# FoX queries and keys made token-major and turned through DRAM, in a two-layer mLSTM and FoX trunk

## The chip, the cores and the metric

The kernel runs on one core of one Trainium2 chip. The metric is device time in microseconds (us) of one execution; the times shown are of separate executions of the same program. A profile is one more execution, recorded by the hardware profiler. Engines are named as the profile does: PE is TensorE (PEld its weight loads), DVE is VectorE, ACT is ScalarE, POOL is GpSimd, SP is SyncE, whose queue issues nearly all loads.

## The reference

The input is x, 256 tokens by 2048 features in float32, with one conditioning vector c. Layer 0 mixes tokens with an mLSTM, layer 1 with FoX attention; each mixer is followed by a SwiGLU FFN (5632 wide). Before every mixer and FFN stands an RMSNorm with a scale and a shift that are computed from c, and every result is added to x through a gate computed from c. What the change touches most is the FoX mixer:

```
def forgetting_attention(q, k, v, log_f):          # 16 heads of 128
    cum = jnp.cumsum(log_f, axis=-1)
    s = jnp.einsum('bhqd,bhkd->bhqk', qi, kf) * scale + cqi[..., None] - cum[..., None, :]
    s = jnp.where(kpos[None, :] <= qpos[:, None], s, -jnp.inf)
    p = jax.nn.softmax(s, axis=-1)
    return jnp.einsum('bhqk,bhkd->bhqd', p, vf)

def fox_mixer(h, w_in, b_f, w_out):
    proj = h @ w_in                                # 2048 -> q, k, v of 2048 each, 16 gates
    ...
    return o.astype(h.dtype) @ w_out
```

and, at the very start, the modulation of layer 0, `mod = silu(c) @ ada_w + ada_b` with `h = rms_norm(x) * (1 + sc1) + sh1`.

## The kernel before, in words

**Products in three parts.** Every large product is a float32 product made of float32r matmuls. A weight block (four k tiles of 128 rows, 512 columns, 1 MB) is loaded by SP into a buffer `raw` (five of them), and in two halves ScalarE writes its rounded part `hi` (line 261) and VectorE the remainder `lo` (line 262); there are four buffers of each, so two blocks can be split ahead. The activations are kept feature-major as `hT`, for each k tile 256 columns of high parts and then 256 of low parts. A product is high x high + high x low + low x high.

**Two shapes of projection.** `group_a` (through `mm_a` and `mm_t`, lines 288 to 290) is token-major: activations are the weights of TensorE, the 512 weight columns move, and for each k tile there are two token halves of three matmuls of 512 columns; its result lies in two PSUM banks. `group_b` (through `mm_b`, lines 271 and 274) is feature-major: for each of four 128-column blocks the weights are stationary, and one matmul of 512 columns (hi against both parts of `hT`) and one of 256 (lo against the high part) follow; its result lies in four of the six banks of that pool, and `total` (lines 353, 355, 357) adds the two halves of a bank. Before the change, FoX q and k use `group_b`, because the score of a head needs q and k with features on the partitions; all other projections use `group_a`.

**Steps and ticks.** Small work is put in the list `steps`, and after each block of four k tiles `tick(n, adv)` takes `adv` steps from it; `drain()` takes all. The same tick lets `bg` start modulation tiles (`ada_tile`: a 1 MB load and one multiply-and-sum on VectorE, line 193) at a rate `FR` per tick. The tile scheduler then sets the order of each engine's queue; only the start, up to the first token-major products, is ordered by hand.

**A FoX head is three steps.** The score (lines 676, 681, 1201): logit bias and mask as bfloat16 matmuls, then q against k in plain float32, into one of the two `aux` banks; VectorE takes the maximum (1211), ScalarE the exponential (1216), VectorE the division by the sum (1223). The flip (922, 923): three 128 x 128 transposes of the weights through an aux bank. The mix (1233, 1236): values against weights, split into high and low for the output projection (362, 363). Four heads form a group, one for each projection of 512 columns of q and of k; their twelve steps are interleaved, all scores first. They become steps as soon as the group's k is there, and run in the ticks of the next projections, one a tick; before the next group's heads are added, `drain()` takes what is left. The output projection `project_out` takes two steps a tick and drains all before its k tile 12, since k tile h is head h.

**The last FFN's turn.** In layer 1 the hidden activations are turned without TensorE: VectorE transposes 32 x 32 squares (line 1128), POOL writes the result to a DRAM tile `aside` (1132) and reads it back rearranged (1136), and ScalarE and VectorE split it (1147, 1148) reading columns 16 bytes apart.

**The start.** SP loads x, then modulation tiles for scale and shift of each k tile, and, between them, 512 KB pairs of k tiles of the first four mLSTM projections (line 780). For k = 0 to 2 the unsplit activations (VectorE line 737, ScalarE line 741) go against unsplit weights in plain float32 (`full_k`, line 785); k = 3 is the first in three parts. `split_act` (362, 363) makes the high and low halves of each `hT` tile, `split_last` (797, 798) those of the weights for k = 3.

## Time and profile before

| what | us |
|---|---|
| three timed executions | 2286.4, 2284.6, 2287.0; median 2286.4 |
| profiled execution | 2287.6, its span 2285.6 |
| TensorE busy in the span | 2259.6 (99%) |
| VectorE, ScalarE, GpSimd busy | 1642.5, 1133.3, 53.8 |
| modulation tiles on VectorE (line 193, 192 of them) | 438.9 |
| low halves of weights on VectorE (line 262, 764) | 925.7 |

The busy time of TensorE counts matmuls whose durations overlap: one of 512 columns is listed with 391 ns, while the next begins after some 230. How fast TensorE goes is therefore read from starts in the timeline, and where it waits from the idle time in brackets behind an instruction. `PEclk` is the clock granted to TensorE as a share of full speed. In the windows view the columns are: stretch, its length, and for each engine the busy time with the number of instructions, then PEclk, the DMA engines' busy share and GB/s.

### The profile page before, as it was taken

To read this page: it belongs to the slowest core of one execution; us is meant where nothing else is said; L and a number is where in the kernel's file an instruction comes from. 1 tells how busy PE (TensorE), PEld (TensorE's weight loads), DVE (VectorE), ACT (ScalarE), POOL (GpSimd) and SP (SyncE) were. 2 spreads that over 40 slices of the span, in tenths; PEclk is the share of its full clock that TensorE was granted. 3 is DMA by queue.
4 is the path that set the end of the run, shared out by engine and by line. 5 is a ranking of instruction groups with operands and counts; after the bars stand their busy time and mean duration, and the time that the engine had idled before them with its cause. 6 is when DMAs were issued, how large, how long until landed. Compare 5 with 4: busy or idle time off the path is not lost.

```text
span 2285.6 us, 26531 instructions
## 1 busy us (share of the span) xinstructions
PE 2259.6 (99%) x10290; PEld 1853.0 (81%) x10290; DVE 1642.5 (72%) x1855; ACT 1133.3 (50%) x1493; POOL 53.8 (2%) x106
## 2 busy tenths in 40 slices
PE   8999999999999999999999999999999999999998
PEld 4877878888888888888888888888888888888886
DVE  7998789878877877865687777777666555555564
ACT  4778564555543344444554544455444443444443
POOL 1000000000000000000000000000010100010000
PEclk9999999999999999999999999999999999999999
DMA  9998989798888889985567878675787665566662
GB/s 386 369 354 332 350 307 355 281 342 336 324 330 332 323 332 342 340 299 185 212 251 277 310 261 293 240 271 195 256 288 254 221 204 189 198 226 217 206 228 104
DMA packets 91809, 635.44 MB, mean 278 GB/s; under 512 B 10962, under 2 KB 11410, under 8 KB 17316
## 3 DMA queue, kind: packets, MB, share of 16 engines
q1 hardware_dynamic: 86400, 617.79, 73.9%
q0 software_dynamic: 5136, 15.83, 2.4%
q8 instruction: 80, 1.31, 0.2%
q14 instruction: 45, 0.37, 0.0%
q10 hardware_dynamic: 148, 0.14, 0.0%
HBM read 625.82 MB, written 7.90 MB: 277 GB/s over the span
## 4 chain that ended last, share of the span: by engine, by line
PE 87%; DVE 6%; DMA 4%; ACT 2%; issue 1%; SPq 0%; POOL 0%; ACTq 0%; DVEq 0%; POOLq 0%
PE mm L290 25%; PE mm L289 25%; PE mm L288 25%; PE mm L271 5%; DMA ada<-in_ada_w_dram 3%; DVE ada L193 3%; PE mm L274 3%; DVE lo L262 2%; ACT hi L261 1%; PE aux L345 1%; PE aux L974 0%; PE aux L483 0%; PE aux L1201 0%; PE mm L554 0%; PE mm L550 0%
## 5 line engine op out<-in xcount | busy, mean ns | idle before, releaser
L262 DVE TENSOR_TENSOR lo<-raw,hi 128x1024 fp32r<-128x1024 f32 x764 | 925.7, 1223 | 488.6 <-ACT hi L261 487.9
L261 ACT CAST hi<-raw 128x1024 fp32r<-128x1024 f32 x764 | 795.6, 1052 | 881.3 <-PE mm L290 780.7
L289 PE MATMUL mm<-lo,hT 128*128 128x512 f32 x1846 | 721.1, 391 | 4.5 <-DVE lo L262 4.5
L288 PE MATMUL mm<-hi,hT 128*128 128x512 f32 x1846 | 720.4, 392 | 1.3 <-ACT hT L362 1.3
L290 PE MATMUL mm<-hi,hT 128*128 128x512 f32 x1846 | 720.8, 390 | 0.0
L193 DVE SCALAR_TENSOR_TENSOR ada<-ada,cs 128x2048 f32<-128x2048 f32 x192 | 438.9, 2286 | 52.4 <-DMA ada<-in_ada_w_dram 52.0
L289 PEld LDWEIGHTS mm<-lo,hT 128*128 128x128 f32 x1846 | 346.9, 188 | 79.1 <-DVE lo L262 8.6
L288 PEld LDWEIGHTS mm<-hi,hT 128*128 128x128 f32 x1846 | 346.6, 188 | 73.5 <-ACT hT L362 2.1
L290 PEld LDWEIGHTS mm<-hi,hT 128*128 128x128 f32 x1846 | 346.7, 188 | 72.7 <-issue 0.5
L288 PE MATMUL mm<-hi,slot 128*128 128x512 f32 x960 | 375.5, 391 | 0.2 <-ACT slot L1007 0.2
L289 PE MATMUL mm<-lo,slot 128*128 128x512 f32 x960 | 374.6, 390 | 0.0
L290 PE MATMUL mm<-hi,slot 128*128 128x512 f32 x960 | 374.6, 391 | 0.0
L290 PEld LDWEIGHTS mm<-hi,slot 128*128 128x128 f32 x960 | 180.3, 188 | 37.8 <-issue 0.7
L288 PEld LDWEIGHTS mm<-hi,slot 128*128 128x128 f32 x960 | 180.3, 188 | 37.7 <-ACT slot L1007 0.8
L289 PEld LDWEIGHTS mm<-lo,slot 128*128 128x128 f32 x960 | 180.4, 188 | 36.9
L271 PE MATMUL mm<-hT,hi 128*128 128x512 f32 x512 | 181.8, 402 | 0.9 <-DVE slot L357 0.9
L274 PE MATMUL mm<-hT,lo 128*128 128x256 f32 x512 | 138.4, 281 | 0.0
L271 PEld LDWEIGHTS mm<-hT,hi 128*128 128x128 f32 x512 | 94.5, 188 | 20.8 <-DVE slot L357 1.3
L274 PEld LDWEIGHTS mm<-hT,lo 128*128 128x128 f32 x512 | 96.8, 189 | 3.1
L829 ACT ACTIVATE slot<-mm 128x512 f32<-128x512 f32 x78 | 45.2, 595 | 39.2 <-PE mm L290 37.4
L1148 DVE TENSOR_TENSOR slot<-slot,slot 128x512 fp32r<-128x512 f32 x22 | 23.8, 1089 | 24.1 <-ACT slot L1147 24.1
L433 ACT ACTIVATE t<-X 128x512 f32<-128x512 f32 x32 | 20.1, 629 | 38.4 <-DVE X L428 38.4
(220 smaller groups left out, 1034.1 us busy)
## 6 DMA issues: line engine op xcount, KB each, us to landing
ada<-in_ada_w_dram SPq DMA_DIRECT2D x192, 1024.0 KB, 6.5
raw<-in_gate_up_dram SPq DMA_DIRECT2D x176, 1024.0 KB, 5.0
raw<-in_down_dram SPq DMA_DIRECT2D x88, 1024.0 KB, 4.8
raw<-in_fox_in_dram SPq DMA_DIRECT2D x48, 1024.0 KB, 4.9
raw<-in_w_in_dram SPq DMA_DIRECT2D x44, 1024.0 KB, 7.4
raw<-in_w_out_dram SPq DMA_DIRECT2D x16, 1024.0 KB, 6.5
raw<-in_fox_out_dram SPq DMA_DIRECT2D x16, 1024.0 KB, 4.9
aside<-slot POOLq DMA_DIRECT2D x22, 256.0 KB, 2.7
```

What stands on the lines that cost most here:

```text
L193: nc.vector.scalar_tensor_tensor(out=raw, in0=raw, scalar=1.0, in1=cs, op0=ALU.mult, op1=ALU.mult, accum_out=acc[layer][:, j : j + 1],)
L261: nc.scalar.copy(hi, raw[:, j : j + 2, :])
L262: nc.vector.tensor_tensor(lo, raw[:, j : j + 2, :], hi.bitcast(F32), op=ALU.subtract)
L271: nc.tensor.matmul(ps, hi, rhs, start=first, stop=last, skip_group_check=True)
L274: nc.tensor.matmul(ps[:, T:], lo, rhs[:, :T], start=False, stop=False, skip_group_check=True)
L288: nc.tensor.matmul(ps, a, hi, start=first, stop=False, skip_group_check=True)
L289: nc.tensor.matmul(ps, a, lo, start=False, stop=False, skip_group_check=True)
L290: nc.tensor.matmul(ps, b, hi, start=False, stop=last, skip_group_check=True)
L345: nc.tensor.transpose(ps[:, j * T + t * P : j * T + (t + 1) * P], src[:, t, (2 * i + j) * P : (2 * i + j + 1) * P], ident,)
L433: nc.scalar.activation(t512(), X[:, t, 512 * i : 512 * (i + 1)], AF.Square, accum_out=self.ss[:, t, i : i + 1],)
L829: nc.scalar.activation(SP[i][:, t, :], banks[t], func)
L1148: nc.vector.tensor_tensor(dst[:, :, T:], ps, dst[:, :, :T].bitcast(F32), op=ALU.subtract)
```

## The change

It does four things. (1) FoX q and k are projected token-major by `group_a`. ScalarE copies each token half out of its bank, with the scale; VectorE transposes its 32 x 32 squares; POOL writes them to DRAM and reads them back with four DMAs into a tile of 256 tokens by 4 heads on 128 feature partitions, the head innermost. The heads' score matmuls read that tile directly, so consecutive tokens of one head are 16 bytes apart. `blocks` and `gather` are the last FFN's functions, moved out. (2) A group's heads become steps only after the next group's q projection, and run in the next k projection, three steps a tick. The last v projection moves behind the last k, and the last heads run after it. (3) In the FoX output projection the first two column groups do k tiles 0 to 11 each, holding four banks, with two steps a tick; then what is left is drained and both do k tiles 12 to 15. (4) At the start, the low half of `hT` for k = 0 to 3 is made behind the next modulation tile's multiply instead of ahead of it, and the weight pairs are fetched in another order among the modulation tiles.

Three places in the engines' queues show it. The first is SP's queue at the start, before the change; `ada` is a modulation tile, `slot<-in_w_in_dram` a weight pair.

```order
L192 DMA ada_232<-in_ada_w_dram 128x2048
L780 DMA slot_242<-in_w_in_dram 128x1024
L780 DMA slot_244<-in_w_in_dram 128x1024
L780 DMA slot_246<-in_w_in_dram 128x1024
L780 DMA slot_248<-in_w_in_dram 128x1024
L192 DMA ada_258<-in_ada_w_dram 128x2048
L192 DMA ada_262<-in_ada_w_dram 128x2048
L192 DMA ada_280<-in_ada_w_dram 128x2048
L192 DMA ada_284<-in_ada_w_dram 128x2048
```

And with the change:

```order
L192 DMA ada_232<-in_ada_w_dram 128x2048
L806 DMA slot_241<-in_w_in_dram 128x1024
L806 DMA slot_243<-in_w_in_dram 128x1024
L192 DMA ada_245<-in_ada_w_dram 128x2048
L806 DMA slot_250<-in_w_in_dram 128x1024
L192 DMA ada_252<-in_ada_w_dram 128x2048
L806 DMA slot_261<-in_w_in_dram 128x1024
L192 DMA ada_279<-in_ada_w_dram 128x2048
L192 DMA ada_284<-in_ada_w_dram 128x2048
```

Modulation tile 2 (`ada_258`, now `ada_245`) has moved ahead of two pairs and tile 3 ahead of one; from tile 4 on the bytes ahead are the same, up to a swap of one pair with tile 6.

The second is VectorE's queue there, for k = 1, before the change (`mods` is one column of scale or shift, `t` the scaled activations, `hT` the low half):

```order
L363 TENSOR_TENSOR hT<-t_36_238,hT 128x256
L193 SCALAR_TENSOR_TENSOR ada_258,acc_124<-ada_258,cs 128x2048
L181 SCALAR_TENSOR_TENSOR mods_122<-acc_124,prm 128x1
L193 SCALAR_TENSOR_TENSOR ada_262,acc_124<-ada_262,cs 128x2048
L187 TENSOR_TENSOR mods_122<-acc_124,prm 128x1
L737 SCALAR_TENSOR_TENSOR t_43_266<-slot_130,mods_122,R 128x256
L363 TENSOR_TENSOR hT<-t_44_268,hT 128x256
L193 SCALAR_TENSOR_TENSOR ada_280,acc_124<-ada_280,cs 128x2048
```

And with the change:

```order
L193 SCALAR_TENSOR_TENSOR ada_245,acc_124<-ada_245,cs 128x2048
L759 TENSOR_TENSOR hT<-t_36_238,hT 128x256
L181 SCALAR_TENSOR_TENSOR mods_122<-acc_124,prm 128x1
L193 SCALAR_TENSOR_TENSOR ada_252,acc_124<-ada_252,cs 128x2048
L187 TENSOR_TENSOR mods_122<-acc_124,prm 128x1
L752 SCALAR_TENSOR_TENSOR t_42_256<-slot_130,mods_122,R 128x256
L193 SCALAR_TENSOR_TENSOR ada_279,acc_124<-ada_279,cs 128x2048
L759 TENSOR_TENSOR hT<-t_43_258,hT 128x256
```

The low half has moved behind the next tile's multiply.

The third is TensorE's queue around a head's score in the FoX stage, before the change (one score between blocks of a feature-major projection):

```order
L676 LDWEIGHTS sel
L676 MATMUL aux_9744<-u_1682_9245,sel 128x512
L681 LDWEIGHTS identb
L681 MATMUL aux_9744<-mask,identb 128x2x128
L1201 MATMUL aux_9744<-slot_9446,slot_9254 128x128
L1201 MATMUL aux_9744<-slot_9446,slot_9254 128x256
L271 MATMUL mm_9698<-hT,hi_9761 128x512
```

And with the change, the third score of a group, four matmuls behind the first two scores, and then the fourth score with two flips behind it (lines 691, 696 and 1241 are the score, 958 the flip):

```order
L288 MATMUL mm_9780<-hi_9866,hT 128x512
L289 MATMUL mm_9780<-lo_9867,hT 128x512
L290 MATMUL mm_9780<-hi_9866,hT 128x512
L288 MATMUL mm_9781<-hi_9866,hT 128x512
L691 LDWEIGHTS sel
L691 MATMUL aux_9846<-u_1682_9245,sel 128x512
L696 LDWEIGHTS identb
L696 MATMUL aux_9846<-mask,identb 128x2x128
L1241 MATMUL aux_9846<-slot_9562,slot_9399 128x128
L1241 MATMUL aux_9846<-slot_9562,slot_9399 128x256
```

```order
L1241 MATMUL aux_9898<-slot_9562,slot_9399 128x128
L1241 MATMUL aux_9898<-slot_9562,slot_9399 128x256
L958 MATMUL aux_9913<-ident,slot_9822 128x128 x3
L288 MATMUL mm_9780<-hi_9929,hT 128x512
L289 MATMUL mm_9780<-lo_9930,hT 128x512
L290 MATMUL mm_9780<-hi_9929,hT 128x512
L958 MATMUL aux_9918<-ident,slot_9837 128x128 x3
L288 MATMUL mm_9781<-hi_9929,hT 128x512
```

Scores and flips of one group stand closer together, in one projection instead of two.

The diff:

```
--- before.py
+++ after.py
@@ -314,7 +314,8 @@
             late.pop(0)()
 
     def group_a(
-        w, c0, act, bgn, adv=1, ka=0, kb=KT, row0=0, seed=None, banks=None, before=None, each=None
+        w, c0, act, bgn, adv=1, ka=0, kb=KT, row0=0, seed=None, banks=None, before=None, each=None,
+        more=False,
     ):
         begun = banks is not None or seed is not None
         if banks is None:
@@ -330,7 +331,7 @@
             if each:
                 each(k)
             for j, (hi, lo) in enumerate(ws):
-                mm_a(banks, hi, lo, act(k + j), not begun and k + j == ka, k + j == kb - 1)
+                mm_a(banks, hi, lo, act(k + j), not begun and k + j == ka, k + j == kb - 1 and not more)
             tick(bgn, adv)
         return banks
 
@@ -347,6 +348,20 @@
                     src[:, t, (2 * i + j) * P : (2 * i + j + 1) * P], ident,
                 )
         return ps.rearrange("p (k t) -> p k t", t=T)
+
+    def blocks(dst, src, aside):
+        nc.vector.transpose(
+            dst.rearrange("p (j b m) -> p j m b", j=4, m=4),
+            src.rearrange("p (m j b) -> p j m b", m=4, j=4),
+        )
+        nc.gpsimd.dma_start(aside, dst)
+
+    def gather(whole, aside):
+        for j in range(4):
+            nc.gpsimd.dma_start(
+                whole[32 * j : 32 * j + 32].rearrange("a (g b) m -> a g (b m)", b=32),
+                aside.rearrange("t (i a) c -> a (t i) c", a=32)[:, :, j * P : (j + 1) * P],
+            )
 
     def total(ps, out, scale=None):
         b = t256()
@@ -739,12 +754,23 @@
         )
         full[k] = f = t256()
         nc.scalar.activation(f, t1, AF.Identity, bias=b)
-        split_act(f, hT[:, k, :])
+        dst = hT[:, k, :]
+        nc.scalar.copy(dst[:, :T], f)
+        lows.append(lambda: nc.vector.tensor_tensor(
+            dst[:, T:], f, dst[:, :T].bitcast(F32), op=ALU.subtract
+        ))
+
+    lows = []
+
+    def lower():
+        while lows:
+            lows.pop(0)()
 
     def early():
         for k in range(KT):
             for vec in (SC1, SH1):
                 ada_tile(0, vec, k)
+                lower()
                 if k == 0 and vec == SC1:
                     row_scale()
                 set_mods(0, vec, k, 1)
@@ -787,32 +813,42 @@
                     start=k == 0, stop=False, skip_group_check=True,
                 )
 
-    def split_last(i):
+    def high_last(i):
         if i % 2 == 0:
-            fine[i // 2] = [
+            fine.append([
                 splitp.tile([P, 2, 512], F32R, tag=g, name=nm(g)) for g in ("hi", "lo")
-            ]
-        hi, lo = (h[:, i % 2, :] for h in fine[i // 2])
-        src = raws[i, 1][:, 1, :]
-        nc.scalar.copy(hi, src)
-        nc.vector.tensor_tensor(lo, src, hi.bitcast(F32), op=ALU.subtract)
-        pairs.append((hi, lo))
-
-    fine, pairs = {}, []
+            ])
+        pairs.append([h[:, i % 2, :] for h in fine[-1]])
+        nc.scalar.copy(pairs[i][0], raws[i, 1][:, 1, :])
+
+    def low_last(i):
+        hi, lo = pairs[i]
+        nc.vector.tensor_tensor(lo, raws[i, 1][:, 1, :], hi.bitcast(F32), op=ALU.subtract)
+
+    fine, pairs = [], []
     upto(1)
-    for i in range(FIRST):
+    for i in (0, 1):
         fetch_pair(i, 0)
+    next(gen)
+    fetch_pair(2, 0)
+    next(gen)
+    fetch_pair(3, 0)
     full_k(0)
-    upto(2)
     full_k(1)
     upto(3)
-    for i in range(2):
+    fetch_pair(0, 2)
+    next(gen)
+    fetch_pair(1, 2)
+    for i in (0, 1):
+        high_last(i)
+        low_last(i)
+    next(gen)
+    assert at[0] == 4
+    lower()
+    for i in (2, 3):
         fetch_pair(i, 2)
-        split_last(i)
-    upto(4)
-    for i in range(2, FIRST):
-        fetch_pair(i, 2)
-        split_last(i)
+        high_last(i)
+        low_last(i)
     full_k(2)
     for i in range(FIRST):
         mm_a(vbanks[i], *pairs[i], h_act(3), False, True)
@@ -1028,9 +1064,15 @@
 
             steps.append(flip)
             return o
-        o = slot().rearrange("p (k t) -> p k t", t=T)
-        group_b(w, KT, c0, h_act, lambda m, ps: total(ps, o[:, m, :], scale), bgn, adv)
-        return o
+        banks = group_a(w, c0, h_act, bgn, adv)
+        whole = slot().rearrange("p (t m) -> p t m", m=4)
+        aside = dram.tile([2, P, 512], F32, tag="aside", name=nm("aside"))
+        for t in range(2):
+            own, turned_own = t512(), t512()
+            nc.scalar.activation(own, banks[t], AF.Copy, scale=1.0 if scale is None else scale)
+            blocks(turned_own, own, aside[t])
+        gather(whole, aside)
+        return whole.rearrange("p t m -> p m t")
 
     for i in range(1, 4):
         unit(i, start[i], KT, LR[0])
@@ -1056,9 +1098,15 @@
 
     def project_out(wo, res, bgn, adv, upto, norm, w2, heads):
         act = lambda k: act_tile(y, k)
+        first = {}
+        if upto == 12:
+            for i in range(2):
+                first[i] = group_a(wo, 512 * i, act, bgn, adv, kb=upto, more=True)
+            drain()
         for i in range(3):
             res.both(i, group_a(
-                wo, 512 * i, act, bgn, adv, before=lambda k: drain() if k >= upto else None
+                wo, 512 * i, act, bgn, adv, ka=upto if i in first else 0, banks=first.get(i),
+                before=lambda k: drain() if k >= upto else None,
             ))
         return bridge(wo, 0, KT, 1536, act, res, 3, norm, w2, heads)
 
@@ -1125,18 +1173,10 @@
                 aside = dram.tile([2, P, 512], F32, tag="aside", name=nm("aside"))
 
             def turn(t):
-                nc.vector.transpose(
-                    squares[:, t, :].rearrange("p (j b m) -> p j m b", j=4, m=4),
-                    sg[:, t, :].rearrange("p (m j b) -> p j m b", m=4, j=4),
-                )
-                nc.gpsimd.dma_start(aside[t], squares[:, t, :])
+                blocks(squares[:, t, :], sg[:, t, :], aside[t])
 
             def spread():
-                for j in range(4):
-                    nc.gpsimd.dma_start(
-                        whole[32 * j : 32 * j + 32].rearrange("a (g b) m -> a g (b m)", b=32),
-                        aside.rearrange("t (i a) c -> a (t i) c", a=32)[:, :, j * P : (j + 1) * P],
-                    )
+                gather(whole, aside)
 
             def flip(i):
                 acts[first + i] = dst = new_act()
@@ -1262,17 +1302,19 @@
     )
     nc.vector.tensor_scalar(cum, cum, -1.0, None, op0=ALU.mult)
     u3 = split3(cum, 16, new)
+    heads = []
     for i in range(4):
         if i == 1:
             vals[2] = keep_v(group_a(w, 2 * D + 1024, h_act, FR, ka=12, banks=begun[2 * D + 1024]))
-        if i == 2:
-            vals[3] = keep_v(group_a(w, 2 * D + 1536, h_act, FR, 2))
         q = keep_t(512 * i, FR, P ** -0.5, layer_w=1)
-        k = keep_t(D + 512 * i, FR, layer_w=1)
+        steps.extend(heads)
+        k = keep_t(D + 512 * i, FR, None, 3, layer_w=1)
         drain()
-        steps.extend(interleave(*[
+        heads = interleave(*[
             fox_head(4 * i + j, q[:, j, :], k[:, j, :]) for j in range(4)
-        ]))
+        ])
+    vals[3] = keep_v(group_a(w, 2 * D + 1536, h_act, FR))
+    steps.extend(heads)
     res = Residual(1, G1, True)
     norm = Norm(res, 1, SC2, SH2)
     begun = project_out(fox_out, res, FR, 2, 12, norm, gate_up[1], [0, DFF, 512])
```

## The prediction

> **What bounds the kernel now.** I read the page first (busy time, then the chain that ended last), then windows over the stage that is rewritten, then the timeline of TensorE inside it, and last the chain of waits of the first 60 us.
>
> ```profile
> span 2285.6 us, 26531 instructions
> PE 2259.6 (99%) x10290; PEld 1853.0 (81%) x10290; DVE 1642.5 (72%) x1855; ACT 1133.3 (50%) x1493; POOL 53.8 (2%) x106
> PE 87%; DVE 6%; DMA 4%; ACT 2%; issue 1%; SPq 0%; POOL 0%; ACTq 0%; DVEq 0%; POOLq 0%
> ...
> 0.00:45.00 45.00, 36.08 (x90) 18.26 (x90) 29.86 (x46) 16.34 (x32) 4.77 (x21) 1.00 0.98 387
> 45.00:214.00 169.00, 166.75 (x736) 135.76 (x735) 148.12 (x175) 128.07 (x199) 2.51 (x4) 1.00 0.96 358
> 1222.00:1452.00 230.00, 229.07 (x1287) 196.68 (x1286) 172.31 (x242) 110.87 (x187) 0.00 (x0) 1.00 0.77 280
> ```
>
> TensorE sets the pace at the full granted clock (1.00). In the FoX projections (1222 to 1452) it is idle for 0.9 of 230 us, while VectorE has 58 us free and the DMA engines 23%. So what this stage is worth is the distance from one matmul's start to the next, and any time by which TensorE waits. Only the first 45 us are set by something else: there the DMA share is 0.98.
>
> **Feature-major against token-major.** The page's mean durations mislead here: 402 and 281 ns for L271 and L274 against 391 ns for L288 would make 20 us of the change. Matmuls overlap, so I take starts.
>
> ```profile
> 1218.61 3.79 PE L665 MATMUL mm<-hT,slot 128*128 128x512 f32 x16
> 1222.24 0.39 PE L271 MATMUL mm<-hT,hi 128*128 128x512 f32 x1
> ...
> 1379.03 0.48 PE L271 MATMUL mm<-hT,hi 128*128 128x512 f32 x1
> ...
> 1407.36 0.39 PE L676 MATMUL aux<-u,sel 96*128 96x512 bf16 x1
> ...
> 1379.10:1407.30 28.20, 28.20 (x162) 24.43 (x160) 20.68 (x24) 11.27 (x16) 0.00 (x0) 1.00 0.81 294
> ```
>
> Sixteen 512-column matmuls take 1222.24 - 1218.61 = 3.63 us, 0.227 us each. From 1379.03 to 1407.36 run 160 matmuls of L271 and L274 (the window counts two more that still run at its edges): five blocks of four k tiles in 28.33 us, 5.67 us a block. A token-major block of four k tiles is 4 x 2 x 3 = 24 matmuls of 512 columns, 24 x 0.227 = 5.45 us; the columns are the same 12,288, but eight matmuls fewer. Eight projections have 32 blocks: 32 x 0.22 = **7.0 us less**.
>
> ```profile
> 1248.76 0.51 PE L271 MATMUL mm<-hT,hi 128*128 128x512 f32 x1 [0.93 <-DVE slot L357]
> ```
>
> Here a new feature-major projection wants four of the six PSUM banks and waits until L357 has emptied one. A token-major one wants two. **0.9 us less**, or nothing if the same late VectorE is met elsewhere.
>
> **The turn.** Per projection the change removes four ScalarE copies and four VectorE adds of 256 columns and adds two ScalarE copies of 512, two VectorE block transposes, two writes to DRAM and four reads back.
>
> ```profile
> L353 ACT ACTIVATE t<-mm 128x256 f32<-128x256 f32 x32 | 12.2, 381 | 17.7 <-PE mm L271 17.7
> L357 DVE SCALAR_TENSOR_TENSOR slot<-mm,t 128x256 f32<-128x256 f32 x16 | 6.5, 420 | 1.0 <-ACT t L353 0.7
> L1128 DVE STREAM_TRANSPOSE slot<-slot 128x512 f32<-128x512 f32 x22 | 23.5, 1080 | 0.0
> L829 ACT ACTIVATE slot<-mm 128x512 f32<-128x512 f32 x78 | 45.2, 595 | 39.2 <-PE mm L290 37.4
> aside<-slot POOLq DMA_DIRECT2D x22, 256.0 KB, 2.7
> slot<-aside POOLq DMA_DIRECT2D x44, 128.0 KB, 5.5
> ```
>
> VectorE: 2 x 1.08 - 4 x 0.42 = +0.5 us a projection, 4 us in 230 where 58 are free. ScalarE: 2 x 0.60 - 4 x 0.38, less than before. Both cost nothing while the high and low halves are split ahead. The transposes wait in VectorE's queue for ScalarE's copies, those for the projection's last matmul, and the low halves of a later block stand behind them; TensorE would notice only if it overtook the block that is already split, 5.45 us, where the two transposes take 2.2. The trip from the last matmul to a usable tile is about 0.6 + 1.1 + 1.1 + 0.6 (issue) + 2.7 + 4 x 0.6 + 5.5 = 14 us. It would stand bare on the path if the heads ran at once; one projection later there are 4 x 5.45 = 21.8 us to cover it. Price nothing; if POOL's queue or the 128 KB reads took 8 us longer, four groups would lose what is over. The traffic, 8 x 1 MB written and read in 230 us, adds 36 GB/s to 280, below the 387 of the first window.
>
> **Heads three steps a tick.** The four heads of a group now come as 12 steps in the four ticks of one k projection, so a third score, or a flip right behind a score, needs one of the two aux banks before the head in it is exponentiated.
>
> ```profile
> 1460.25 0.39 PE L676 MATMUL aux<-u,sel 96*128 96x512 bf16 x1
> ...
> 1461.24 0.38 PE L676 MATMUL aux<-u,sel 96*128 96x512 bf16 x1
> 1461.44 0.62 DVE L1211 TENSOR_REDUCE den<-aux 128x1 f32<-128x128 f32 x2 [1.01 <-PE aux L1201]
> ...
> 1462.87 0.20 ACT L1216 ACTIVATION_READ_ACCUMULATOR slot<-aux,den 128x1 f32 x1
> ...
> 1476.88 0.93 PE L922 MATMUL aux<-ident,slot 128*128 128x128 f32 x6
> 1477.57 0.48 PE L289 MATMUL mm<-lo,slot 128*128 128x512 f32 x1
> 1478.00 0.70 PE L1233 MATMUL aux<-slot,slot 128*128 128x256 f32 x2
> ```
>
> A score takes TensorE 0.99 us (1460.25 to 1461.24) and its bank is free after 1463.07 - 1460.25 = 2.8 us; a flip takes 0.35 (two between 1476.88 and 1477.57). The third score stands behind two scores and four matmuls, 0.99 + 0.99 + 0.91 = 2.9 us after the first began: no wait. The second flip stands behind the fourth score, a flip and three matmuls (0.68): 2.0 us, so it waits 0.8, and all that is behind it on TensorE waits too. Three groups: **+2.4 us**. Ends: 0 (the flip gets the other bank) and +9.3, if each time a 2.3 us reduction of a modulation tile (L193 below) runs on VectorE ahead of the maximum.
>
> **The output projection in pieces** leaves the number of matmuls alone; six ticks of two steps replace three ticks and a drain of six steps at once. In that drain starts are lengthened, as from 1477.57 to 1478.00 (0.43 instead of 0.23); for six steps I take **-0.3**, ends 0 and -1.2.
>
> **The strided q and k.** The gathered tile keeps the head innermost, so the score matmuls read q as weights and k as moving columns 16 bytes apart. No row of TensorE shows that. The nearest are the two engines that read such a tile in the last FFN:
>
> ```profile
> L1147 ACT CAST slot<-slot 128x512 fp32r<-128x512 f32 x22 | 24.1, 1108 | 16.3 <-DMA slot<-aside 16.3
> L1147 ACT CAST slot<-aux 128x512 fp32r<-128x512 f32 x22 | 12.6, 580 | 3.2 <-PE aux L345 3.2
> L362 ACT CAST slot<-aux 128x256 fp32r<-128x256 f32 x16 | 5.7, 374 | 5.3 <-PE aux L1236 5.3
> L1148 DVE TENSOR_TENSOR slot<-slot,slot 128x512 fp32r<-128x512 f32 x22 | 23.8, 1089 | 24.1 <-ACT slot L1147 24.1
> L1148 DVE TENSOR_TENSOR slot<-aux,slot 128x512 fp32r<-128x512 f32 x22 | 14.9, 684 | 0.0
> L1201 PE MATMUL aux<-slot,slot 128*128 128x256 f32 x32 | 9.6, 381 | 0.0
> L1201 PE MATMUL aux<-slot,slot 128*128 128x128 f32 x32 | 6.1, 274 | 0.0
> ```
>
> ScalarE goes from (580 - 374) / 256 = 0.80 ns an element to 0.80 + 528 / 512 = 1.83; VectorE loses 405 / 512 = 0.79 ns an element, to about 1.8. A score column in fp32 costs TensorE (381 - 274) / 128 = 0.84 ns, while the same engine takes a 4-byte column of L665 in 227 / 512 = 0.44 ns. If the stride costs a factor of about two, as it does to the two engines together, 0.44 becomes 0.89 against the 0.84 that fp32 needs anyway: 0.05 x 768 columns (a score is two matmuls of 128 and two of 256, 64 in all) x 16 heads = **+0.6 us**. If instead it is an absolute 1.83 ns, it is (1.83 - 0.84) x 768 x 16 = +12.2 us. The ends are 0 and +12.2; I take the first reading because it rests on TensorE's own reading speed, and the second is the main rival.
>
> The Trainium skill, page "Advanced Engine Details and Errata", section "SBUF Cachelines", speaks against the change: lines are 16 bytes, at least two hits on a line are needed to hide the access, and a different line for each access is penalised. The rows of ScalarE and VectorE agree, 1.83 ns against 0.80; whether it reaches an fp32 matmul no row shows. By that rule the sum is the rival's.
>
> **The first 45 us.**
>
> ```profile
> 23.33 2.31 DVE ada L193 x2
> ...
> 29.27 0.41 ACT hT L362
> 29.71 0.43 DVE hT L363
> ...
> 44.13 0.41 ACT hT L362
> 44.59 0.51 PE mm L288
> ...
> 29.29 5.42 PE L785 MATMUL mm<-slot,t 128*128 128x512 f32 x12 [3.82 <-ACT t L741]
> 39.62 0.30 PEld L785 LDWEIGHTS mm<-slot,t 128*128 128x128 f32 x2 [0.59 <-DMA slot<-in_w_in_dram]
> ```
>
> The chain runs through VectorE, which at k = 0 to 2 stands still for the hi half (L362, 0.41) and then makes the low half (L363, 0.43) before it may take the next modulation tile. Now the low half comes after that tile, and tiles 2 and 3 are fetched ahead of two and one of the 512 KB weight pairs. At 387 GB/s a pair is 1.35 us: tile 3 lands that much earlier, and full_k(1) starts near 28.0 instead of 29.29. The chain to the k = 3 norm (44.13 to 44.54) also sheds 0.41 + 0.43 at k = 1 and 2, so the norm is ready between 41.5 and 42.9. But the bytes ahead of the last weight pairs are the same: full_k(2) still waits at 39.62 for its third pair, and the eight matmuls from there, 5.42 / 12 = 0.45 us each, end at 43.2. There the k = 3 matmuls follow at once: 44.59 - 43.2 = **1.4 us less**; ends 0 (the next stage, 45 to 214, with a DMA share of 0.96, absorbs it) and -1.7.
>
> **Sum.** -7.0 - 0.9 + 2.4 - 0.3 + 0.6 - 1.4 = -6.6 us. The profiled execution took 2287.6 us (2.0 around its span of 2285.6) and would take 2281.0; the median of the three timed runs is 2286.4, 1.2 us less, so the median becomes **2279.8 us**.
>
> **Rivals.** *The stride is an absolute rate.* One mechanism, in the 64 score matmuls: 2279.8 - 0.6 + 12.2 = 2291.4, slower than before. It decides from about 1.43 ns a column (0.84, and the other terms' 7.2 us over 768 x 16 columns), where it has eaten the gain. For it: two engines of different natural speed end at the same 1.8 ns, which looks like a limit of the memory and not of the engine. Against it: TensorE reads twice as fast as either in contiguous data.
>
> *The clump takes the place of the projection's gain.* With VectorE late at every second flip, +9.3 instead of +2.4: 2286.7, no change. For it: VectorE is 75% busy there and takes its queue in order. Against it: it sat idle before the maximum in the rows above (1.01 us).
>
> *The DRAM trip is late*, 14 us becoming over 22 plus the wait of POOL's queue: 5 us in each of the four groups, 2299.8. Against it stand the 5.5 us landings of the same reads with the same queues.
>
> **How the numbers follow.** Forecast 0.48; absolute stride 0.32; clump 0.16; late trip 0.04. A difference under 0.2%, 4.6 us, can't be told from none here. The forecast's own range is 2276 to 2283, and 0.41 of its 0.48 lies below 2281.8, with 0.02 of the clump: faster 0.42. The absolute stride straddles 2291.0: just over half of it slower, with the late trip 0.21. The rest, 0.37, is no change. The range from 2275.5 to 2292 leaves out some 0.2.
>
> **What would show it.** In the profile after: eight projections under the token-major lines with starts 0.227 us apart and none of L271's form; the score matmuls at 274 and 381 ns (near 370 and 570 if the rival is right) and the next matmul's start behind them; TensorE's idle time before flips in three clumps; the first matmul of L288 at about 43.2 us; no wait that a read of the turned tile ends. I am wrong if scores lengthen, if TensorE's idle in the stage grows beyond 3 us, or if the q and k tiles end waits.

## The result, and the profile after

The change made the kernel slower: 2304.6 us median of six executions (2297.7 to 2309.6) against 2285.7 us before, a ratio of 1.008 with a 95% interval of 1.0063 to 1.0097. The forecast was 2279.8 us, with a range that ended at 2292.0.

The profiled execution took 2307.1 us. First its page, then the stretch that was 230 us of unbroken work before (columns as ahead: length, then PE, PEld, DVE, ACT, POOL, PEclk, DMA share, GB/s).

```profile
span 2304.9 us, 26107 instructions
PE 2274.6 (99%) x10034; PEld 1850.4 (80%) x10034; DVE 1646.3 (71%) x1839; ACT 1135.4 (49%) x1477; POOL 81.6 (4%) x154
...
1222.00:1452.00 230.00, 221.83 (x956) 177.12 (x955) 166.30 (x219) 104.96 (x165) 25.40 (x44) 0.98 0.82 285
```

In these 230 us TensorE is now idle for 8.2 us, where it was 0.9, and its granted clock is 0.98, where it was 1.00. The "99%" of the page does not tell this. I cut the run at two matmuls that both kernels have: the last one of the gate product, which opens the FoX stage, and the first transpose behind the output projection, which closes it.

| us | before | after | difference |
|---|---|---|---|
| start to the FoX stage | 1222.0 | 1219.1 | -3.0 |
| FoX stage | 328.3 | 349.8 | +21.5 |
| behind it, to the last matmul | 726.2 | 727.1 | +0.8 |

So the start gains, the stage that was rewritten loses, and little happens elsewhere. (The table is of one profiled execution each. Six other profiles, of kernels that are the same as one of the two up to the stage, enter it up to 1.5 us away from these, so a difference of about 1 us means little.) Three things in the stage answer to the prediction. First the score matmuls and their weight loads, by form, over the stage:

```profile
L1241 PE MATMUL aux<-slot,slot 128*128 128x256 f32 x32 | 17.5, 636 | 0.0
L1241 PEld LDWEIGHTS aux<-slot,slot 128*128 128x128 f32 x64 | 16.2, 326 | 2.0 <-issue 0.3
L1241 PE MATMUL aux<-slot,slot 128*128 128x128 f32 x32 | 11.5, 450 | 0.0
```

636 and 450 ns stand where 381 and 274 stood, and a weight load takes 326 ns where it took 192:

```profile
L1201 PEld LDWEIGHTS aux<-slot,slot 128*128 128x128 f32 x64 | 8.4, 192 | 1.9
```

Second, the waits of TensorE, from its timeline:

```profile
1285.65 0.80 PE L289 MATMUL mm<-lo,hT 128*128 128x512 f32 x1 [2.59 <-DVE lo L262]
...
1305.05 0.39 PE L288 MATMUL mm<-hi,hT 128*128 128x512 f32 x1
1307.49 0.38 PE L691 MATMUL aux<-u,sel 96*128 96x512 bf16 x1 [2.06 <-ACT slot L1256]
...
1367.43 0.57 PE L691 MATMUL aux<-u,sel 96*128 96x512 bf16 x1 [2.14 <-ACT slot L1256]
```

The first is a low half that VectorE has not made yet; the other two are third scores of a group, the place for which the prediction said "no wait". Ahead of the first and of the last, VectorE had stood still for a modulation tile, for 6.05 and 2.77 us:

```profile
1282.16 2.29 DVE L193 SCALAR_TENSOR_TENSOR ada<-ada,cs 128x2048 f32<-128x2048 f32 x1 [6.05 <-DMA ada<-in_ada_w_dram]
...
1363.55 2.29 DVE L193 SCALAR_TENSOR_TENSOR ada<-ada,cs 128x2048 f32<-128x2048 f32 x1 [2.77 <-DMA ada<-in_ada_w_dram]
```

What held the exponential (L1256) at 1307 stands in the queues of VectorE and ScalarE:

```profile
1300.04 2.29 DVE L193 SCALAR_TENSOR_TENSOR ada<-ada,cs 128x2048 f32<-128x2048 f32 x1 [1.79 <-DMA ada<-in_ada_w_dram]
...
1302.26 2.36 DVE L262 TENSOR_TENSOR lo<-raw,hi 128x1024 fp32r<-128x1024 f32 x2
1304.53 0.62 DVE L1251 TENSOR_REDUCE den<-aux 128x1 f32<-128x128 f32 x2
...
1305.23 1.28 ACT L1256 ACT_TABLE_LOAD   x1 [3.26 <-DVE den L1251]
1306.53 0.37 ACT L1256 ACTIVATE slot<-aux,den 128x128 f32<-128x128 f32 x1
```

VectorE waited 1.79 us for a modulation tile to land, then had two low halves in its queue, and only then the maximum; ScalarE, idle for 3.26 us, then loaded its table before the exponential. Third, the DMA issues between 1240 and 1470 us (the last number is the median from issue to landing). Before:

```profile
raw<-in_fox_in_dram SPq DMA_DIRECT2D x29, 1024.0 KB, 4.9
ada<-in_ada_w_dram SPq DMA_DIRECT2D x24, 1024.0 KB, 4.9
```

After:

```profile
raw<-in_fox_in_dram SPq DMA_DIRECT2D x28, 1024.0 KB, 7.4
ada<-in_ada_w_dram SPq DMA_DIRECT2D x22, 1024.0 KB, 6.6
...
aside<-t POOLq DMA_DIRECT2D x16, 256.0 KB, 5.1
slot<-aside POOLq DMA_DIRECT2D x32, 128.0 KB, 7.5
```

Weights and modulation tiles land 2.5 and 1.7 us later than before, although the bytes moved in these 230 us rose only from 281 to 292 GB/s. The five `raw` buffers make this a ring: SP may issue a load only when VectorE has freed a buffer (in these 230 us it waits 52.4 us for a multiply by VectorE before it issues a modulation tile, where it was 22.6), and VectorE, which takes its queue in order, stands still until the load has landed.

### The profile page after: what moved, and what is told of

The parts are those of the page before. It is cut to its first block, busy times and chain, and to the rows that moved or that the text cites. A ratio compares the mean times of both kernels' runs of the same rounds, so it can differ in the third digit from the quotient of the medians.

```text
span 2304.9 us, 26107 instructions
## 1 busy us (share of the span) xinstructions
PE 2274.6 (99%) x10034; PEld 1850.4 (80%) x10034; DVE 1646.3 (71%) x1839; ACT 1135.4 (49%) x1477; POOL 81.6 (4%) x154
## 3 DMA queue, kind: packets, MB, share of 16 engines
q8 instruction: 78, 1.28, 0.2%
## 5 line engine op out<-in xcount | busy, mean ns | idle before, releaser
L289 PE MATMUL mm<-lo,hT 128*128 128x512 f32 x2102 | 823.5, 392 | 8.5 <-DVE lo L262 8.5
L288 PE MATMUL mm<-hi,hT 128*128 128x512 f32 x2102 | 822.9, 393 | 0.0
L290 PE MATMUL mm<-hi,hT 128*128 128x512 f32 x2102 | 821.3, 391 | 0.0
L289 PEld LDWEIGHTS mm<-lo,hT 128*128 128x128 f32 x2102 | 396.0, 188 | 95.3 <-DVE lo L262 13.5
L290 PEld LDWEIGHTS mm<-hi,hT 128*128 128x128 f32 x2102 | 395.6, 188 | 82.9 <-issue 1.0
L288 PEld LDWEIGHTS mm<-hi,hT 128*128 128x128 f32 x2102 | 395.5, 188 | 82.5 <-issue 0.5
L288 PE MATMUL mm<-hi,slot 128*128 128x512 f32 x960 | 375.6, 391 | 0.2 <-ACT slot L1043 0.2
L288 PEld LDWEIGHTS mm<-hi,slot 128*128 128x128 f32 x960 | 180.3, 188 | 37.9 <-ACT slot L1043 0.8
L865 ACT ACTIVATE slot<-mm 128x512 f32<-128x512 f32 x78 | 45.2, 596 | 39.7 <-PE mm L290 38.0
L361 POOL DMA_DIRECT2D slot<-aside x76 | 44.5, 592 | 98.0 <-DMA aside<-slot 41.9
L357 POOL DMA_DIRECT2D aside<-slot x22 | 12.4, 564 | 633.5 <-DVE slot L353 633.5
L1164 ACT ACTIVATE slot<-mm 128x512 f32<-128x512 f32 x44 | 25.6, 599 | 15.4 <-PE mm L290 14.8
L443 DVE TENSOR_TENSOR X<-X,t 128x512 f32<-128x512 f32 x48 | 32.3, 687 | 0.6
```

What stands on the lines that cost most here:

```text
L288: nc.tensor.matmul(ps, a, hi, start=first, stop=False, skip_group_check=True)
L289: nc.tensor.matmul(ps, a, lo, start=False, stop=False, skip_group_check=True)
L290: nc.tensor.matmul(ps, b, hi, start=False, stop=last, skip_group_check=True)
L361: nc.gpsimd.dma_start(whole[32 * j : 32 * j + 32].rearrange("a (g b) m -> a g (b m)", b=32), aside.rearrange("t (i a) c -> a (t i) c", a=3 ...
L443: nc.vector.tensor_tensor(cols, cols, m, op=ALU.add)
L865: nc.scalar.activation(SP[i][:, t, :], banks[t], func)
```

## The experiments

Three theories came out of this: (S) the strided scores, (T) the late landings that the trip through DRAM causes, with the waits behind them, and (C) the clump of heads by itself. All ratios are to the kernel before, run on the same chip.

**The stride alone, in the kernel before.** The order in which VectorE writes q and k is the only change.

```
-        o = slot().rearrange("p (k t) -> p k t", t=T)
+        o = slot().rearrange("p (t k) -> p k t", t=T)
```

> The kernel before, with nothing changed but the order in which VectorE writes the q and k tiles: head innermost, so that the scores read 16 bytes apart. Theory (the stride by itself costs 0.8 us a head): 2285.7 + 13 = 2298 to 2301, scores at about 450 and 636 ns. Rival (the stride costs only where scores stand in a clump of four, the matmuls around them hide it otherwise): under 3 us, below 2289.

Measured: 2302.1 us, ratio 1.0065 (1.0048 to 1.0082), some 15 us. The stage of the profiled execution grew from 328.3 to 341.7 us, so 13.4 us are the stride's:

```profile
L1202 PE MATMUL aux<-slot,slot 128*128 128x256 f32 x32 | 17.5, 635 | 0.0
...
L1202 PE MATMUL aux<-slot,slot 128*128 128x128 f32 x32 | 11.6, 452 | 0.0
```

Theory S holds, also without a clump or a trip: 0.84 us a head.

**k in runs of 32 tokens, then q contiguous too, in the changed kernel.** VectorE writes its squares head by head, so that the gathered k has runs of 128 bytes; in the second kernel ScalarE also copies q head by head, one projection later. (The code is shortened here.)

```
-            dst.rearrange("p (j b m) -> p j m b", j=4, m=4),
+            dst.rearrange("p (j m b) -> p j m b", j=4, m=4),      # k only
...
+        steps.append(lambda: nc.scalar.copy(dst, src))           # q, second kernel only
```

> The change, with k alone made nearly contiguous: VectorE writes its squares head by head, so a head's k lies in runs of 32 tokens (128 bytes); q stays 16 bytes apart. Theory (a strided read costs TensorE an absolute time for each column, mostly as moving columns): the 256-column score matmul falls from 636 to about 380 ns, the 128-column one from 450 to about 275, and the median from 2304.6 by 9 to 12 us to 2293 to 2296. Rival (the weights are what costs, and the score matmuls wait for their slow loads, 326 instead of 192 ns): matmuls stay over 600 ns and the time within 3 us of 2304.6.

> As the one with k in runs, and q copied head by head by ScalarE one projection later, so that no score reads a strided tile. Theory: scores at 274 and 381 ns, weight loads at 192, four scores' lengthening of about 0.8 us a head gone, 13 to 15 us less than with the change: 2290 to 2292. Rival (waits of the clump and of VectorE are what costs, and they take back what the scores give): less than 5 us, 2300 or more.

Measured: 2307.3 us, ratio 1.0075 (1.0049 to 1.0101), with k in runs; 2303.5 us, ratio 1.0069 (1.0054 to 1.0084), with both. The scores did what theory S says, the time did not. With k in runs:

```profile
L1243 PEld LDWEIGHTS aux<-slot,slot 128*128 128x128 f32 x64 | 16.1, 325 | 1.9
...
L1243 PE MATMUL aux<-slot,slot 128*128 128x256 f32 x32 | 12.1, 462 | 0.0
...
L1243 PE MATMUL aux<-slot,slot 128*128 128x128 f32 x32 | 10.1, 397 | 0.0
```

And with both:

```profile
L1243 PEld LDWEIGHTS aux<-slot,slot 128*128 128x128 f32 x64 | 9.2, 206 | 2.1 <-issue 0.3
...
L1243 PE MATMUL aux<-slot,slot 128*128 128x256 f32 x32 | 10.5, 412 | 0.0
L1243 PE MATMUL aux<-slot,slot 128*128 128x128 f32 x32 | 6.6, 291 | 0.0
...
1307.30 0.38 PE L691 MATMUL aux<-u,sel 96*128 96x512 bf16 x1 [3.06 <-ACT slot L1258]
```

Both operands cost: from the first matmul of a score to the one behind it the 64 score matmuls take 20.0 us in the changed kernel, 15.2 with k in runs and 9.8 with both (8.2 before the change). But with both contiguous the third scores wait 3.06 and 3.19 us instead of 2.06 and 2.14: a faster TensorE reaches the same late VectorE earlier. Of the expected 13 us only 4.3 are gained in the stage (345.5 instead of 349.8); longer waits took back the rest of what the scores gave, as the rival had it. The trace of the first kernel says little of its time: it is of an execution of 2295.8 us, inside what its theory expected, while the other three took 2306.9 to 2308.8, and what these waited for isn't on record.

**Heads two steps a tick, in the changed kernel**, the last four of a group in the next q projection.

```
-        k = keep_t(D + 512 * i, FR, None, 3, layer_w=1)
-        drain()
+        k = keep_t(D + 512 * i, FR, None, 2, layer_w=1)
```

> The change, with the heads two steps a tick in the k projection and the last four steps in the ticks of the next q projection, instead of three a tick and a drain. Theory (the third scores' waits, 2.2 and 2.3 us, and the fall of TensorE's clock that follows each idle, some 3.2 us, come from the clump): no wait of over 1 us before a score, clock 1.00 there, 7 to 8 us less: about 2297. Rival (the clock falls for another reason, such as the long scores themselves): the waits go but the clock still falls to about 0.5 at the scores, some 4.5 us less: 2300.

Measured: 2304.8 us, ratio 1.0081 (1.0064 to 1.0098): nothing gained. Both expectations missed. The waits moved from the third scores to low halves (1.66 us at 1408, 1.76 at 1464) and to later scores (1.48 at 1476). That heads come in a clump is not the cause as it stands.

**The heads alone, in the kernel before**: one projection behind, three steps a tick, q and k as they were.

```
-        k = keep_t(D + 512 * i, FR, layer_w=1)
+        steps.extend(heads)
+        k = keep_t(D + 512 * i, FR, None, 3, layer_w=1)
```

> The kernel before with only the heads moved: one projection behind, three steps a tick in the next k projection, the last v projection behind the last k. q and k stay feature-major and contiguous, there is no trip through DRAM. Theory (the third score's wait needs the late VectorE that the trip's loads cause): under 2 us more, up to 2288. Rival (the clump makes the wait by itself, with the load of the exponential's table and the fall of the clock behind it): 5 to 7 us more, 2291 to 2293.

Measured: 2290.5 us against 2289.1, ratio 1.0009 (1.0000 to 1.0018), between 0 and 4 us. There is one wait of 1.10 us before a third score, and the stage takes 331.4 us, 3.1 more. The clump costs about what the prediction gave it (2.4 us), in another place.

**The start alone, in the kernel before**: part (4) of the change, the late low halves and the other order of the weight pairs.

```
-        split_act(f, hT[:, k, :])
+        nc.scalar.copy(dst[:, :T], f)
+        lows.append(lambda: nc.vector.tensor_tensor(
...
-    for i in range(FIRST):
+    for i in (0, 1):
         fetch_pair(i, 0)
+    next(gen)
+    fetch_pair(2, 0)
+    next(gen)
+    fetch_pair(3, 0)
     full_k(0)
```

> The kernel before with only the start of the change. Theory (the 2.3 us by which the first matmul of L288 came earlier last to the end): 2283 to 2284. Rival (the next stage, whose DMA share is 0.97, takes them back): 2285.5 to 2286.

Measured: 2285.6 us against 2289.1, ratio 0.9991 (0.9982 to 1.0000). The FoX stage begins at 1219.3 instead of 1222.0: the gain lasts, as the theory had it.

**Fewer bytes, then less work, for the modulation tiles of the last FFN, in the changed kernel.** The first loads a quarter of each tile and multiplies it four times, the second loads all and multiplies a quarter; the modulation values are wrong in both.

```
-        nc.sync.dma_start(raw, ada_w[layer, j])
+        nc.sync.dma_start(raw[:, : D // 4], ada_w[layer, j][:, : D // 4])   # first kernel
...
-            out=raw, in0=raw, scalar=1.0, in1=cs, op0=ALU.mult, op1=ALU.mult,
+            out=raw[:, :n], in0=raw[:, :n], scalar=1.0, in1=cs[:, :n],      # second, n = D // 4
```

> The change, but of the 48 modulation tiles for the last FFN, most of which load in the FoX stage, only a quarter of the bytes is loaded, and VectorE multiplies that quarter four times, so that its work stays the same; the values of those tiles are therefore wrong and the output with them. Theory (the DMA engines are overloaded, 0.91 busy where they were 0.84, a modulation tile lands late, and VectorE's queue, with the low halves and the maxima, stands behind it): no wait for a low half at about 1265 and 1283, third scores wait under 1 us, 6 to 8 us less than the change: 2296 to 2299; the scores stay long. Rival (the order of VectorE's queue makes the waits, not the loads): waits as before, 2302 or more.

> The change, with the 48 modulation tiles for the last FFN loaded in full, but VectorE multiplies only a quarter of each (0.7 instead of 2.3 us); these modulation values and the output are therefore wrong. Theory (late landings make the waits: five buffers in a ring, SP waits for VectorE to free one, VectorE for the tile to land): VectorE still idle over 25 us for modulation tiles between 1240 and 1470, waits for low halves at about 1265 to 1290 stay, 2299 or more. Rival (VectorE's own work makes it late): waits under 3 us in all, 2293 to 2297.

Measured: 2301.7 us, ratio 1.0057 (1.0044 to 1.0071), and 2297.0 us, ratio 1.005 (1.0034 to 1.0066). Neither took the waits away: of 9.4 us (waits of 0.5 us and more in the stage) 9.1 and 4.9 were left. The first group's third score, with a quarter of the bytes:

```profile
1309.80 0.59 PE L700 MATMUL aux<-u,sel 96*128 96x512 bf16 x1 [5.45 <-ACT slot L1265]
```

And with a quarter of the work:

```profile
1304.27 0.38 PE L692 MATMUL aux<-u,sel 96*128 96x512 bf16 x1 [2.93 <-ACT slot L1257]
```

In the kernel with a quarter of the bytes the DMA share was 0.58 to 0.74 over windows of 30 us from 1222 to 1462, where it was 0.73 to 0.91 with the change, and weights and tiles landed after 5.4 and 4.6 us. So a lower mean load of the DMA engines doesn't take the waits away, and less work of VectorE takes half of them. The first kernel is no clean test of the bytes, though: its four multiplies hold VectorE for some 2.8 us a tile, where the one of the change takes 2.2. VectorE goes on standing still for these tiles; its idle time until one landed, and how often, between 1240 and 1470 us, for the kernel before, the change, a quarter of the bytes and a quarter of the work, in this order:

```profile
  DMA ada<-in_ada_w_dram: 25.5, 15
```

```profile
  DMA ada<-in_ada_w_dram: 33.4, 15
```

```profile
  DMA ada<-in_ada_w_dram: 28.8, 14
```

```profile
  DMA ada<-in_ada_w_dram: 38.7, 16
```

A quarter tile of 256 KB took 4.6 us to land, hardly less than 1 MB before (4.9): it seems to wait behind other transfers more than for its own bytes. That the second kernel gained 7 us of the stage (342.8 instead of 349.8; the first 1.4) says that VectorE's work is a part of the ring all the same.

**No trip through DRAM, in the changed kernel.** VectorE writes its squares straight into the tile that the scores read; no write, no read back. What the trip does besides, to move the squares between partitions, is left out, so the scores read wrong values.

```
-            blocks(turned_own, own, aside[t])
-        gather(whole, aside)
+            nc.vector.transpose(
+                whole[:, t * P : (t + 1) * P, :].rearrange("p (j b) m -> p j m b", j=4),
+                own.rearrange("p (m j b) -> p j m b", m=4, j=4),
+            )
```

> The change without its trip through DRAM: VectorE writes its squares straight into the tile that the scores read (as strided as before, with wrong values, so the output is wrong); no write to DRAM and no read back. Theory (the trip's traffic makes the modulation tiles and weights land late, 6.6 and 7.4 us instead of 4.9, and that makes the waits): landings at about 4.9, no wait over 1.5 us in the FoX projections, clock 1.00, as with early modulation tiles: 2294 to 2297, the strided scores alone left. Rival (shorter blocks and the clump make the waits, the trip only rides along): waits of 2 us before third scores and for low halves stay, 2301 or more.

Measured: 2295.0 us, ratio 1.0026 (1.0015 to 1.0038). This is the run that decides, and its theory held. Landings, and VectorE's idle time for modulation tiles:

```profile
raw<-in_fox_in_dram SPq DMA_DIRECT2D x29, 1024.0 KB, 4.8
ada<-in_ada_w_dram SPq DMA_DIRECT2D x24, 1024.0 KB, 4.8
```

```profile
  DMA ada<-in_ada_w_dram: 6.5, 10
```

```profile
1301.91 0.38 PE L691 MATMUL aux<-u,sel 96*128 96x512 bf16 x1 [0.26 <-ACT slot L1257]
```

The third score waits 0.26 us instead of 2.06, though clump, blocks and stride are as they were. The stage takes 336.2 us instead of 349.8: **13.6 us are the trip's**, theory T (12 by the medians, each against the kernel before on its chip). Which part of the trip makes the loads late, its bytes, its many small pieces or its queue, no run separates, and no run changed the number of buffers in the ring.

**The modulation tiles early.** The tiles for scale and shift of the last FFN are started in the first FFN, and 0.2 instead of 0.66 a tick in the FoX stage: in the changed kernel, in the kernel before, and in the changed kernel with contiguous q and k.

```
             want(1, G1)
+            want(1, SC2, SH2)
...
-    want(1, SC2, SH2)
...
-    r0=(0.75, 0.7, 0.8, 0.5), fr=0.66, r1=(0.3, 0.3, 0.3, 0.3))
+    r0=(0.75, 0.7, 0.8, 0.5), fr=0.2, r1=(0.3, 0.3, 0.3, 0.3))
```

> The change with its strided q and k, and only the modulation tiles for the last FFN started earlier and at 0.2 a tick in the FoX stage. Theory (the stride costs its 13 us of the stage wherever TensorE does not wait for something else): 2295 to 2298, waits in the stage under 5 us in all, scores still at 450 and 636 ns. Rival (stride and waits replace each other, so that taking the waits away gives nearly all back): 2286 to 2290.

> The kernel before with only the modulation tiles for the last FFN moved earlier, at 0.2 a tick in the FoX stage. Theory (before the change TensorE waits 1.6 us in the stage in all, so there is nothing to gain): 2285 to 2287, no change. Rival (these tiles moved early, not the token-major projections, made the fast version): 2281 to 2283.

> The one with no strided score, and the modulation tiles for the last FFN started earlier, in the down projection of the first FFN where the DMA share is 0.57 to 0.68, at 0.2 instead of 0.66 a tick in the FoX stage. Theory (strided scores and overloaded DMA engines are the two causes): waits of the FoX stage under 6 us in all where they were 19.8, clock 1.00, 2281 to 2286. Rival (the clump's order on VectorE and ScalarE is the second cause): waits stay over 10 us, 2295 or more.

Measured: 2295.3 us, ratio 1.0035 (1.0022 to 1.0048); 2298.3 us, ratio 1.0047 (1.0033 to 1.0061); and 2283.2 us, ratio 0.9981 (0.9972 to 0.9990). With fewer modulation tiles in the ring the waits are gone although the trip and the clump are there, as the theories of the first and the third kernel had it: the stage takes 336.3 us with the stride, as without the trip, and 323.0 without the stride. The difference of these two, 13.3 us, is the stride again. So it takes the trip and the modulation tiles together to make the waits; without either they are gone. Landings of the first kernel, with the trip:

```profile
raw<-in_fox_in_dram SPq DMA_DIRECT2D x28, 1024.0 KB, 5.6
ada<-in_ada_w_dram SPq DMA_DIRECT2D x7, 1024.0 KB, 4.9
```

The kernel before gets nothing in the stage (327.6 instead of 328.3) and loses 8.3 us behind it in the profiled execution, where the tiles that were put off now crowd; neither side expected that:

```profile
1595.17 0.50 PE L289 MATMUL mm<-lo,hT 128*128 128x512 f32 x1 [1.60 <-DVE lo L262]
```

```profile
1642.60 0.51 PE L288 MATMUL mm<-hi,hT 128*128 128x512 f32 x1 [1.37 <-ACT hi L261]
1643.92 0.50 PE L289 MATMUL mm<-lo,hT 128*128 128x512 f32 x1 [0.81 <-DVE lo L262]
```

**Both causes out, and the tiles where they fit.** The contiguous version with early tiles and heads two steps a tick; and the same with the tiles at 1.0 a tick in the first FFN's last down projection and 0.35 in the FoX stage.

```
-    r0=(0.75, 0.7, 0.8, 0.5), fr=0.2, r1=(0.3, 0.3, 0.3, 0.3))
+    r0=(0.75, 0.7, 0.8, 1.0), fr=0.35, r1=(0.3, 0.3, 0.3, 0.3))
```

> The version with contiguous q and k and early modulation tiles, with its heads two steps a tick in the k projection and the last four in the next q projection. Theory (the one wait left, 1.25 us before the third score, belongs to the clump): no wait over 0.5 us before a score, 1 us less than the version it is made from: 2281 to 2283. Rival (heads that end later meet the next group's on VectorE): new waits of some 2 us, 2284 to 2286.

> The fastest version (contiguous q and k, early modulation tiles, heads two steps a tick), with the modulation tiles at 1.0 a tick in the last down projection of the first FFN and 0.35 in the FoX stage, so that fewer are left for the norm behind it. Theory (what that version lost behind the FoX stage, 733.1 us to the end where the kernel before has 726.2, is a burst of late modulation tiles): no wait over 1.5 us there, 726 to 728 us to the end, 2276 to 2279, the 7 us of the forecast. Rival (the tiles now collide with the FoX stage or the down projection): 2281 to 2284.

Measured: 2281.9 us, ratio 0.9978 (0.9970 to 0.9987), and 2280.9 us, ratio 0.9960 (0.9949 to 0.9972), the fastest of all, though the 2276 to 2279 of its theory was missed. The second takes 724.1 us behind the stage, where the first took 733.1; its stage is 322.2 us. TensorE is idle for 0.6 of 240 us:

```profile
1222.00:1462.00 240.00, 239.38 (x1103) 196.61 (x1102) 159.90 (x209) 124.43 (x185) 27.73 (x48) 1.00 0.78 265
```

The waits behind the stage went, as its theory said, but the tiles that were moved lengthened the time up to the stage from 1218.0 to 1224.4 us; part of the gain was paid for there.

## Why the prediction was wrong

The stage's difference can be put together from the runs: -5.2 us (323.0 against 328.3, without stride and late tiles), +13.3 (the stride: 336.3 against 323.0), +13.4 (the trip's traffic: 349.8 against 336.3). Their sum is the +21.5 of the profile. The split of the last two depends on the order: the other way round the late tiles cost 22.5 us without the stride (345.5 against 323.0), and the stride 4.3 on top of them (349.8 against 345.5). Only their sum, some 27 us, doesn't. The -5.2 holds the early tiles too, which gave the kernel before 0.7. Two of the prediction's own three signs of being wrong came: longer scores, and 8.2 us of idle time in 230.

**Strided q and k: the term was mis-sized.** The step "I take the first reading because it rests on TensorE's own reading speed" failed: +0.6 us stood in the sum, 13.4 was measured, just over the upper end of 12.2. The main rival, an absolute rate, was right in kind, and its 11.6 us more than the forecast were near the measured 12.8, in part by luck. The rows for it were there: ScalarE and VectorE ended at the same 1.8 ns an element. The moving columns alone cost (636 - 450) / 128 = 1.45 ns, below the 1.83 of the rival: (1.45 - 0.84) x 768 x 16 = 7.5 us of the 13.4. The rest lies around them, where the weights load in 326 instead of 192 ns and the next matmul starts later; the rival had left that out. What the Trainium skill's page "Advanced Engine Details and Errata", section "SBUF Cachelines", says of a different line for each access held for both operands of an fp32 matmul. The rival's time, 2291.4, was 13 us too low, since it had no term for what follows.

**The trip's traffic: the step that failed unseen.** "The traffic, 8 x 1 MB written and read in 230 us, adds 36 GB/s to 280, below the 387 of the first window" priced a flow by its mean, and "Price nothing" put the trip at 0 us where 13.4 was measured. The trip itself stayed under its cover, as forecast: no wait ends with a read of q or k. But while it is under way, other loads land 2 us later, the ring of five buffers has no room for that, and VectorE's order carries the delay to the low halves and the maxima. The rival of a late trip (2299.8) looked at the right transfers and at the wrong victims. What the prediction read as VectorE's spare time, 58 us of 230, was in part time in which it stood waiting for modulation tiles: 25.5 us already before.

**Third score: "no wait" failed.** The 2.8 us from a score to its free bank were taken from an exponential that found VectorE free and its table loaded. In the first group 1.28 us of table load and a late VectorE came on top. The second flips, to which +2.4 us were given, wait almost nothing. As the clump's price without the trip, 2.4 us can stand: the heads alone cost 0 to 4 us.

**Matmul form: right; bank wait and pieces not measured alone.** The first token-major projections run without a gap:

```profile
L288 PE MATMUL mm<-hi,hT x49: 389/389/389, 1219.3 to 1251.9; 128*128 128x512 f32 x49
```

48 steps of three matmuls in 32.6 us are 5.43 us a block, as forecast (5.45, where it was 5.67). The terms of the stage without stride, -7.0 - 0.9 + 2.4 - 0.3 = -5.8, stand against the measured -5.2.

**The start: right, and too small.** The first matmul of L288 came at 42.33, not 43.2:

```profile
39.19 1.98 PE L811 MATMUL mm<-slot,t 128*128 128x512 f32 x4 [1.02 <-DMA slot<-in_w_in_dram]
41.01 1.88 PE L811 MATMUL aux<-slot,t 128*128 128x512 f32 x4
42.33 0.79 PE L288 MATMUL mm<-hi,hT 128*128 128x512 f32 x1
```

The third weight pair landed 0.43 us earlier (in other kernels with this start it was up to 0.5 us later than here, so this is within the spread), and the eight matmuls took 3.14 us instead of the 3.6 that I gave them by their listed durations: -2.3 us instead of -1.4, and -2.7 at the stage in the run of the start alone.

With both failed terms out, the forecast was near: the fastest version takes 2280.9 us, 0.40% below the kernel before (0.28 to 0.51%), some 7 us on that chip. It holds a rate of the modulation tiles and a spread of the heads of its own, so it doesn't prove the sum, but it shows that the gain was to be had. (In the chances, 0.41 and 0.02 make 0.43 and not 0.42; nothing hangs on it.)

## What to carry to other kernels

Price a detour through DRAM by what it does to the landing of other loads, not by its mean bandwidth: look up which engine stands still for those loads, how many buffers lie between, and what waits in that engine's queue behind them. Count a strided operand at the rate that the other engines' rows show for such a tile, for weights as well as moving columns, unless a row shows otherwise. And if the removal of one cost changes nothing, look for a second cost that waits underneath: here the stride, taken out while the tiles were late, gave 4.3 us of the stage, and 13.3 once they were not.

## What was not expected of the hardware

TensorE's granted clock fell to half after most idle times of some 2 us, and stayed there for about 3.4 us. One-microsecond windows of the changed kernel, behind the wait that ended at 1307.49:

```profile
1308.00:1309.00 1.00, 1.00 (x5) 0.90 (x5) 0.61 (x3) 0.29 (x2) 0.00 (x0) 1.00 0.98 328
1309.00:1310.00 1.00, 1.00 (x4) 0.57 (x3) 0.51 (x2) 0.62 (x4) 0.00 (x0) 0.73 1.01 303
1310.00:1311.00 1.00, 1.00 (x4) 0.80 (x3) 1.00 (x2) 0.79 (x4) 0.00 (x0) 0.50 1.20 250
1311.00:1312.00 1.00, 1.00 (x4) 0.81 (x3) 1.00 (x1) 0.12 (x2) 0.00 (x0) 0.50 0.91 233
1312.00:1313.00 1.00, 1.00 (x4) 0.76 (x4) 0.46 (x4) 0.16 (x1) 0.00 (x0) 0.56 1.10 291
```

The missing clock adds up to 0.27 + 0.50 + 0.50 + 0.44 = 1.7 us. The sixteen traces hold fourteen waits of 1.92 us and more behind their first 60 us, from 1.92 to 5.45 us. All but two (2.56 and 2.57 us) go with such a fall, which begins between 1 us before the wait's end and 2 us behind it; the one with 5.45 us lost 3.4 us of clock, the others 1.7. Of the shorter ones, the seven from 1.58 to 1.83 us had none, and a single one of 1.48 us had one. Of three pairs of some 1.4 and 0.8 us within 1.4 us, two had one, such as the one at 1642.60 and 1643.92 above; the third, in the changed kernel with q and k contiguous, had none. In the first 60 us it is otherwise: of five waits from 2.01 to 3.82 us in the plain float32 products, only one (3.31 us, with the stride alone) was followed by a fall. The longest is the 3.82 us that the prediction shows at 29.29 in the kernel before, and the clock stayed at 1.00 there. So an idle time of this length often goes with a fall and isn't enough for one; what else decides isn't shown.

In the changed kernel three falls, 5.1 us, and the waits of 0.5 us and more, 9.4 us in the stage, are 14.5 us, about the 13.4 of the trip. That the idle time causes the fall is read from this coincidence and from the runs in which both went together; no run set an idle time by itself.
